# Upper and lower weight products of a chunk in two runs, and norm factors from one rounded product with ones

## The chip, the cores and the metric

The kernel runs on one core of one Trainium2 chip. The metric is the device time of one execution in microseconds, as the median of several runs.

## The reference

The reference is a decoder trunk of two layers over 256 tokens with 2,048 features, in float32. Layer 0 mixes tokens by attention in three dilation groups; layer 1 by a gated sum of compressed, selected-block and window attention, whose keys and values come from the stream after layer 0. After each mixer come an MLP and a gated per-layer embedding:

```
def rmsnorm(x, g):
    y = xf * lax.rsqrt(jnp.mean(xf * xf, axis=-1, keepdims=True) + NORM_EPS)
    return y * g
...
hn = rmsnorm(h, mlp_norm_g[i])
h = h + jnp.square(jax.nn.relu(hn @ mlp_w1[i])) @ mlp_w2[i]
gate = jax.nn.sigmoid(rmsnorm(h, ple_norm_g[i]) @ ple_w_gate[i])
h = h + (p[i] @ ple_w_proj[i]) * gate
```

Here `mlp_w1` is 2,048 x 8,192 and `mlp_w2` 8,192 x 2,048, in each of the two layers.

## The kernel before

The residual stream lies in SBUF feature-major: 16 tiles `x[k]` of 128 features x 256 tokens. All weights come in chunks of 128 x 1,024 float32, and nearly all of the work is multiplying chunks.

To keep float32 precision with rounded (fp32r) products, a weight is split in two: ACT casts the chunk to an upper part `hi` (line 197, tile `whi`) and DVE subtracts it from the raw chunk to make the lower part `lo` (line 203, tile `wlo`). Activations are split as well: a tile `xa` holds the upper half in columns 0 to 255 and the lower half in columns 256 to 511. A chunk is eight blocks of 128 x 128. For each block `mm_tile` issues two products: the upper weights with both halves of the activations (512 columns, line 321), and right behind it the lower weights with the upper half alone (256 columns, line 322). Every product has a weight load of its own. In PSUM a result so has two halves, which `sum_halves` (lines 326 and 328) adds.

Two helpers call `mm_tile`. `quad` takes chunks of two contraction blocks by four output blocks, and so fills four PSUM banks at once; `single` makes one output block from two chunks of eight contraction blocks each, all into one bank. PSUM has four banks named `mm` and two pairs named `at`, between which `four_banks` alternates. The last gate product (`one_half`, lines 376 to 378) uses 256-column products only. Two other helpers have loops of their own: `token_major` (lines 404 to 406), with 512-column products that move weights against activations as the loaded operand, and `compress` (lines 893 and 894), with 256-column ones. `both` lets chunks of these two alternate.

`Program.run` writes the order of all instructions by hand. For each chunk it issues loads (up to seven ahead), casts (four ahead), subtractions (three ahead), then one step of every generator under way, and then the chunk's products. A generator's `yield` means "go on at the next chunk"; `yield "tensor"` means "go on right behind this chunk's products". There are four raw buffers, six of `hi` and five of `lo`.

A norm is not applied to the activations but to the result, as a factor of each token. `Norm` adds up the squares of the 16 tiles into `acc` (128 partitions x 256 tokens); `factor` then makes a column of sums with two 1-column fp32 products (`column`, line 236), takes the root and inverts it on 128 x 2 elements (`root`, `invert`), writes the factors into a diagonal `diag`, spreads them over all partitions by an fp32 product with ones (`spread`, line 260), and copies them out as `r`. Four of the norms, those before the MLP and before the gate in each layer, enter as a hook behind the fifth chunk of the first `quad` that needs them; their results are used as `norm.rb`, first at line 464 (MLP) and line 550 (gate). The others go on to use the column and stay on `factor`.

Of the kernel before, what the change touches and what calls it, by code (L numbers as in the profile page):

```python
# [10 lines left out]
F32 = mybir.dt.float32  # L11
F32R = mybir.dt.float32r
AF = mybir.ActivationFunctionType
ALU = mybir.AluOpType

P = 128
D = 2048
T = 256
KT = D // P
DH = 128  # L20
EPS = 1e-6
# [19 lines left out]
def f32(ap):  # L41
    return ap.bitcast(F32)
# [90 lines left out]
def kernel(ctx: ExitStack, tc: tile.TileContext, a: dict, out: bass.AP):  # L133
    nc = tc.nc
# [3 lines left out]
    const = ctx.enter_context(tc.tile_pool(name="const", bufs=1))  # L138
    xpool = ctx.enter_context(tc.tile_pool(name="x", bufs=1))
    stat = ctx.enter_context(tc.tile_pool(name="stat", bufs=2))  # L140
    tmp = ctx.enter_context(tc.tile_pool(name="tmp", bufs=2))
# [4 lines left out]
    cur = {}  # L146
# [10 lines left out]
    def bank():  # L157
        return pspool.tile([P, 512], F32, tag="mm", name="mm", bufs=4)

    def banks2():  # L160
        return pspool.tile([P, 2, 512], F32, tag="at", name="at", bufs=2)
# [5 lines left out]
    x = [xp[k // 2][:, k % 2 * T:(k % 2 + 1) * T] for k in range(KT)]  # L167
    ones = const.tile([P, P], F32, name="ones")
    nc.vector.memset(ones, 1.0)
    ident = const.tile([P, P], F32, name="ident")  # L170
    ropeC = const.tile([32, T], F32, name="ropeC")
    ropeS = const.tile([32, T], F32, name="ropeS")
# [34 lines left out]
    class Norm:  # L207
# [51 lines left out]
        def spread(self, ps):  # L259
            nc.tensor.matmul(ps[:, 128:128 + T], ones, self.diag, start=True, stop=True)  # L260
            return ps[:, 128:128 + T]

        def factor(self, roped=False):
            while self.done < KT:
                yield
            yield "tensor"
            ps = self.column([self.acc])
            yield
            self.root(ps)
            yield  # L270
            self.invert()
            yield "tensor"
            rp = self.spread(ps)
            yield
            r = stat.tile([P, T], F32, tag="sr", name="sr", bufs=1)
            nc.scalar.copy(r, rp)
            if roped:
                yield
                self.rc = stat.tile([P, T], F32, tag="rc", name="rc", bufs=1)
                self.rs = stat.tile([32, T], F32, tag="rs", name="rs", bufs=1)  # L280
                nc.vector.tensor_mul(self.rs, r[:32, :], ropeS)
                nc.vector.tensor_copy(self.rc, r)
                nc.vector.tensor_mul(self.rc[:32, :], r[:32, :], ropeC)
            self.r = r
# [30 lines left out]
    def have(acts, k):  # L315
        prog.until(lambda: acts[k] is not None)
        return acts[k]

    def mm_tile(ps, hi, lo, col, rhs, first, last):

        nc.tensor.matmul(ps, hi[:, col:col + P], rhs, start=first, stop=False)  # L321
        nc.tensor.matmul(ps[:, :T], lo[:, col:col + P], rhs[:, :T], start=False, stop=last)  # L322

    def sum_halves(ps):
        s = tmp.tile([P, T], F32, tag="es", name="es", bufs=4)
# [5 lines left out]
    parity = [0]  # L331

    def four_banks():
        parity[0] ^= 1
        if parity[0]:
            return [bank() for _ in range(4)]
        return [p[:, i, :] for p in (banks2(), banks2()) for i in range(2)]
# [6 lines left out]
    def quad(src, nk, acts, done, hooks=None, single_ring=False, late=False):  # L344

        st = []
        for c in range(nk // 2):
            def step(hi, lo, c=c):
                if c == 0:
                    st.extend([bank() for _ in range(4)] if single_ring else four_banks())  # L350
                for i in range(2):
                    have(acts, 2 * c + i)
                for f in range(4):
                    for i in range(2):
                        k = 2 * c + i
                        mm_tile(st[f], hi, lo, i * 512 + f * P, acts[k], k == 0, k == nk - 1)
                if c < nk // 2 - 1:
                    return []
                return [delayed(done(f, st[f]), f // 2 if late else 0) for f in range(4)]
            prog.chunk(src(c), step)  # L360
            for fn in (hooks or {}).get(c, ()):
                prog.op(fn)

    def single(src, acts, done, mid=(), ring=bank, one_half=False):

        st = []
        for c in range(2):
            def step(hi, lo, c=c):
                if c == 0:
                    st.append(ring())  # L370
                for i in range(8):
                    k = 8 * c + i
                    if one_half:
                        xg, ps = have(acts, k), st[0][:, :T]
                        wh, wl = hi[:, i * P:(i + 1) * P], lo[:, i * P:(i + 1) * P]
                        nc.tensor.matmul(ps, wh, xg[:, :T], start=k == 0, stop=False)
                        nc.tensor.matmul(ps, wh, xg[:, T:], start=False, stop=False)
                        nc.tensor.matmul(ps, wl, xg[:, :T], start=False, stop=k == KT - 1)
                        continue
                    mm_tile(st[0], hi, lo, i * P, have(acts, k), k == 0, k == KT - 1)  # L380
                return [done(st[0])] if c else []
            prog.chunk(src(c), step)
            if c == 0:
                for fn in mid:
                    prog.op(fn)
# [69 lines left out]
    def mlp(layer, xg, norm, to, norm2):  # L455
        for b in range(NFB):
            h = [None] * 16
            for q in range(4):
                def done(f, ps, q=q, h=h):
                    t = sum_halves(ps)  # L460
                    yield
                    while norm.r is None:
                        yield
                    nc.vector.scalar_tensor_tensor(t, t, 0.0, norm.rb, op0=ALU.max, op1=ALU.mult)
                    yield
                    nc.scalar.activation(t, t, AF.Square)
                    ht = cur["h"].tile([P, 2 * T], F32R, tag="h", name="h", bufs=20)
                    yield from split_to(ht, t)
                    h[4 * q + f] = ht
                base = layer * 128 + (b * 4 + q) * 8  # L470
                quad(lambda c, base=base: a["w1"][base + c], KT, xg, done,
                     {4: [norm.factor]} if b == 0 and q == 0 else None, late=True)
            for q in range(4):
                def done(f, ps, q=q, b=b):
                    k = 4 * q + f
                    add_to_x(k, ps)
                    if b == NFB - 1:
                        yield
                        yield from renorm(k, G_PLE + layer, to, norm2)
                base = layer * 128 + (b * 4 + q) * 8  # L480
                quad(lambda c, base=base: a["w2"][base + c], 16, h, done, late=True)
# [10 lines left out]
    def ple(layer, pg, xg, norm, nxt, norm2, last):  # L492
# [80 lines left out]
        for q in range(4):  # L573
            def proj_done(f, ps, q=q):
                s = tmp.tile([P, T], F32, tag="es", name="es", bufs=4)
                nc.scalar.copy(s, ps[:, :T])
                t = cur["h"].tile([P, T], F32, tag="pj", name="pj", bufs=8)
                nc.vector.tensor_add(t, ps[:, T:], s)
                pj[4 * q + f] = t
                return  # L580
                yield
            quad(lambda c, q=q: a["w_proj"][layer * 4 + q], 2, pg, proj_done)
            hooks = {4: [norm.factor]} if q == 0 else {}
            if q == 3 and not last:
                for c in range(6):
                    hooks[c] = [lambda k=k: split_x(k, G_KV, nxt) for k in (2 * c, 2 * c + 1)]
            if q == 3 and last:
                for f in range(4):
                    single(lambda c, f=f: a["w_gl"][2 * f + c], xg,
                           (lambda ps, k=12 + f: gate_done(k, ps)) if f < 3 else last_gate,  # L590
                           ring=last_ring if f == 3 else lambda: banks2()[:, 0, :], one_half=f == 3)
            else:
                quad(lambda c, q=q: a["w_gate"][layer * 32 + q * 8 + c], KT, xg,
                     lambda f, ps, q=q: gate_done(4 * q + f, ps), hooks)
# [143 lines left out]
    hooks = {c: [lambda k=k: start_x(k) for k in (2 * c + 2, 2 * c + 3)] for c in range(7)}  # L738
# [3 lines left out]
    for h in range(HA):  # L742
        for i in range(6):
            single(lambda c, h=h, i=i: a["w_qk"][(h * 6 + i) * 2 + c], x_a0,
                   lambda ps, h=h, i=i: qk_done(h, i, ps),
# [423 lines left out]
    for h in range(HB):  # L1169
# [4 lines left out]
        if h:  # L1174
            prog.op(lambda h=h: b_scores(h - 1))
    hooks = {0: [lambda: b_pv(HB - 4, True), lambda: b_transpose(HB - 3)],
             1: [lambda: b_scores(HB - 1, banks2)],
             2: [lambda: b_pv(HB - 3, True), lambda: b_transpose(HB - 2)],
             4: [lambda: b_pv(HB - 2, True), lambda: b_transpose(HB - 1)],
             5: [lambda: b_pv(HB - 1, True)]}  # L1180
# [107 lines left out]
```

## Time and profile before

| | |
|---|---|
| median of 3 runs | 2519.74 us (2519.64 to 2519.77) |
| the profiled execution | 2519.91 us |
| its span, first to last instruction | 2518.1 us |
| granted TensorE clock, mean | 0.999 |
| busy: PE, PEld, DVE, ACT | 2507.3, 2204.1, 1716.8, 1342.8 us |
| read from HBM | 461.65 MB, 184 GB/s over the span |

PE is TensorE's matrix product, PEld its weight load, DVE the vector engine, ACT the scalar engine. Products are pipelined and overlap, so their busy time is not the time that each adds; the distance between two starts is.

### The profile page before, as it was taken

The numbers are of one execution on the slowest core, as the hardware profiler recorded it, in microseconds if no ns is written. First come the engines' busy times: TensorE is split into PE (matmuls) and PEld (weight loads), VectorE is DVE, ScalarE is ACT, GpSimd is POOL, SyncE is SP. The second block draws the span as 40 slices with busy tenths as digits, with TensorE's granted clock in tenths as the row PEclk, the third lists the DMA queues.
The fourth block names the chain that finished last, engine by engine and source line by source line (L and its number), as shares of the span: only waits on it lengthen the run. The fifth ranks groups of instructions, "written<-read, shape, count | busy, mean of one in ns | idle before, by whom it ended". The sixth has DMA issues, their size and how long they took to land.

```text
span 2518.1 us, 38042 instructions
## 1 busy us (share of the span) xinstructions
PE 2507.3 (100%) x14457; PEld 2204.1 (88%) x14457; DVE 1716.8 (68%) x3000; ACT 1342.8 (53%) x2152; POOL 10.4 (0%) x24
## 2 busy tenths in 40 slices
PE   9999999999999999999999999999999999999998
PEld 8888888888888888888888889888888888888887
DVE  6766677866565665567787989776556656556777
ACT  6444444554454453455564788655435445445555
POOL 0000000000000000000000000000000000000000
PEclk9999999999999999999999999999999999999999
DMA  7555555555555555555565743455555565555653
GB/s 268 173 180 178 175 161 180 176 188 189 193 188 190 192 190 189 190 191 189 185 199 190 248 155 125 141 191 185 192 190 188 191 191 188 190 192 188 190 185 124
DMA packets 130119, 466.23 MB, mean 185 GB/s; under 512 B 14608, under 2 KB 15888, under 8 KB 129936
## 3 DMA queue, kind: packets, MB, share of 16 engines
q1 hardware_dynamic: 129264, 462.68, 56.8%
q8 instruction: 113, 1.85, 0.3%
q0 software_dynamic: 528, 1.07, 0.2%
q14 instruction: 70, 0.57, 0.1%
q10 hardware_dynamic: 144, 0.07, 0.0%
HBM read 461.65 MB, written 2.10 MB: 184 GB/s over the span
## 4 chain that ended last, share of the span: by engine, by line
PE 99%; DVE 0%; DMA 0%; SPq 0%; ACT 0%; issue 0%; DVEq 0%
PE mm L321 31%; PE at L321 26%; PE mm L322 16%; PE at L322 14%; PE mm L404 1%; PE mm L406 1%; PE mm L405 1%; PE at L406 1%; PE at L404 1%; PE at L405 1%; PE at L1135 0%; PE at L673 0%; PE mm L1159 0%; PE mm L893 0%; PE mm L894 0%; DMA raw<-in_w_v 0%
## 5 line engine op out<-in xcount | busy, mean ns | idle before, releaser
L203 DVE TENSOR_TENSOR wlo<-raw,whi 128x1024 fp32r<-128x1024 f32 (+1 forms) x875 | 1065.5, 1219 | 624.8 <-PE at L322 242.1
L197 ACT CAST whi<-raw 128x1024 fp32r<-128x1024 f32 (+1 forms) x875 | 920.4, 1053 | 914.6 <-PE at L321 409.9
L321 PE MATMUL mm<-xa,whi 128*128 128x512 f32 x2176 | 765.1, 395 | 0.0
L322 PE MATMUL mm<-xa,wlo 128*128 128x256 f32 x2176 | 608.1, 279 | 0.0
L321 PE MATMUL at<-xa,whi 128*128 128x512 f32 x1648 | 573.6, 392 | 0.0
L321 PEld LDWEIGHTS mm<-xa,whi 128*128 128x128 f32 x2176 | 407.8, 187 | 91.9 <-issue 0.4
L322 PE MATMUL at<-xa,wlo 128*128 128x256 f32 x1648 | 461.1, 280 | 0.0
L322 PEld LDWEIGHTS mm<-xa,wlo 128*128 128x128 f32 x2176 | 410.6, 189 | 0.4
L321 PEld LDWEIGHTS at<-xa,whi 128*128 128x128 f32 x1648 | 308.3, 187 | 68.0
L321 PE MATMUL at<-h,whi 128*128 128x512 f32 x1024 | 355.7, 391 | 0.0
L321 PE MATMUL mm<-h,whi 128*128 128x512 f32 x1024 | 355.7, 391 | 0.0
L322 PEld LDWEIGHTS at<-xa,wlo 128*128 128x128 f32 x1648 | 311.3, 189 | 0.1
L322 PE MATMUL mm<-h,wlo 128*128 128x256 f32 x1024 | 286.7, 280 | 0.0
L322 PE MATMUL at<-h,wlo 128*128 128x256 f32 x1024 | 286.7, 280 | 0.0
L321 PEld LDWEIGHTS mm<-h,whi 128*128 128x128 f32 x1024 | 191.5, 187 | 42.0
L321 PEld LDWEIGHTS at<-h,whi 128*128 128x128 f32 x1024 | 191.5, 187 | 42.0
L322 PEld LDWEIGHTS mm<-h,wlo 128*128 128x128 f32 x1024 | 193.5, 189 | 0.0
L322 PEld LDWEIGHTS at<-h,wlo 128*128 128x128 f32 x1024 | 193.5, 189 | 0.0
L328 DVE TENSOR_TENSOR et<-mm,es 128x256 f32<-128x256 f32 x137 | 55.8, 422 | 80.3 <-ACT es L326 78.3
L326 ACT COPY es<-mm 128x256 f32<-128x256 f32 x137 | 48.2, 370 | 66.0 <-PE mm L322 63.0
L328 DVE TENSOR_TENSOR et<-at,es 128x256 f32<-128x256 f32 x103 | 43.5, 423 | 36.8 <-ACT es L326 31.3
L326 ACT COPY es<-at 128x256 f32<-128x256 f32 x103 | 37.8, 370 | 51.8 <-DVE et L328 40.5
(301 smaller groups left out, 2387.8 us busy)
## 6 DMA issues: line engine op xcount, KB each, us to landing
raw<-in_w SPq DMA_DIRECT2D x512, 512.0 KB, 3.5
raw<-in_w_qk SPq DMA_DIRECT2D x96, 512.0 KB, 3.7
raw<-in_w_gate SPq DMA_DIRECT2D x56, 512.0 KB, 3.6
raw<-in_w_kv SPq DMA_DIRECT2D x48, 512.0 KB, 4.2
raw<-in_w_v SPq DMA_DIRECT2D x46, 512.0 KB, 3.6
raw<-in_w_q SPq DMA_DIRECT2D x32, 512.0 KB, 4.4
raw<-in_w_oB SPq DMA_DIRECT2D x32, 512.0 KB, 3.6
raw<-in_w_oA SPq DMA_DIRECT2D x16, 512.0 KB, 3.6
```

The source lines that it names most:

```text
L197: nc.scalar.copy(hi[:, c], t[:, c])
L203: nc.vector.tensor_sub(lo[:, c], t[:, c], f32(hi)[:, c])
L321: nc.tensor.matmul(ps, hi[:, col:col + P], rhs, start=first, stop=False)
L322: nc.tensor.matmul(ps[:, :T], lo[:, col:col + P], rhs[:, :T], start=False, stop=last)
L326: nc.scalar.copy(s, ps[:, :T])
L328: nc.vector.tensor_add(t, ps[:, T:], s)
L404: nc.tensor.matmul(st[j], xh, wh, start=k == 0, stop=False)
L405: nc.tensor.matmul(st[j], xl, wh, start=False, stop=False)
L406: nc.tensor.matmul(st[j], xh, wl, start=False, stop=k == KT - 1)
```

## The change

`mm_tile` becomes `mm_tiles`: it takes a chunk's eight blocks as a list and issues all eight products with upper weights first, and then all eight with lower weights. `quad` and `single` hand it the list. `one_half`, `token_major` and `compress` stay as they are.

`factor_rows` is a new way to a norm's factors, for the four norms before the MLPs and the gates. It rounds `acc` on ACT and subtracts on DVE, so that one `h` tile holds an upper and a lower half of 256 columns; one product with a rounded 128 x 128 matrix of ones (512 columns) sums both over the partitions and leaves the sums on all of them; root and inverse are then taken on 128 x 256 elements.

```diff
--- before.py
+++ after.py
@@ -167,6 +167,8 @@
     x = [xp[k // 2][:, k % 2 * T:(k % 2 + 1) * T] for k in range(KT)]
     ones = const.tile([P, P], F32, name="ones")
     nc.vector.memset(ones, 1.0)
+    onesr = const.tile([P, P], F32R, name="onesr")
+    nc.gpsimd.memset(f32(onesr), 1.0)
     ident = const.tile([P, P], F32, name="ident")
     ropeC = const.tile([32, T], F32, name="ropeC")
     ropeS = const.tile([32, T], F32, name="ropeS")
@@ -260,6 +262,30 @@
             nc.tensor.matmul(ps[:, 128:128 + T], ones, self.diag, start=True, stop=True)
             return ps[:, 128:128 + T]
 
+        def factor_rows(self):
+
+            while self.done < KT:
+                yield
+            a = cur["h"].tile([P, 2 * T], F32R, tag="h", name="h", bufs=20)
+            nc.scalar.copy(a[:, :T], self.acc)
+            yield
+            nc.vector.tensor_sub(a[:, T:], self.acc, f32(a[:, :T]))
+            yield "tensor"
+            ps = banks2()[:, 0, :] if parity[0] else bank()
+            nc.tensor.matmul(ps, onesr, a, start=True, stop=True)
+            yield
+            v, z = (tmp.tile([P, T], F32, tag="et", name="et", bufs=7) for _ in range(2))
+            r = stat.tile([P, T], F32, tag="sr", name="sr", bufs=1)
+            nc.vector.tensor_scalar(z, ps[:, :T], 1.0 / D, EPS, op0=ALU.mult, op1=ALU.add)
+            nc.vector.scalar_tensor_tensor(v, ps[:, T:], 1.0 / D, z, op0=ALU.mult, op1=ALU.add)
+            nc.scalar.activation(z, v, AF.Sqrt)
+            yield
+            nc.vector.reciprocal(r, z)
+            nc.vector.tensor_mul(z, r, r)
+            nc.vector.scalar_tensor_tensor(z, z, -0.5, v, op0=ALU.mult, op1=ALU.mult)
+            nc.vector.scalar_tensor_tensor(r, z, 1.5, r, op0=ALU.add, op1=ALU.mult)
+            self.r = r
+
         def factor(self, roped=False):
             while self.done < KT:
                 yield
@@ -316,10 +342,16 @@
         prog.until(lambda: acts[k] is not None)
         return acts[k]
 
-    def mm_tile(ps, hi, lo, col, rhs, first, last):
-
-        nc.tensor.matmul(ps, hi[:, col:col + P], rhs, start=first, stop=False)
-        nc.tensor.matmul(ps[:, :T], lo[:, col:col + P], rhs[:, :T], start=False, stop=last)
+    def mm_tiles(hi, lo, tiles):
+
+
+
+
+
+        for ps, col, rhs, first, last in tiles:
+            nc.tensor.matmul(ps, hi[:, col:col + P], rhs, start=first, stop=False)
+        for ps, col, rhs, first, last in tiles:
+            nc.tensor.matmul(ps[:, :T], lo[:, col:col + P], rhs[:, :T], start=False, stop=last)
 
     def sum_halves(ps):
         s = tmp.tile([P, T], F32, tag="es", name="es", bufs=4)
@@ -350,10 +382,8 @@
                     st.extend([bank() for _ in range(4)] if single_ring else four_banks())
                 for i in range(2):
                     have(acts, 2 * c + i)
-                for f in range(4):
-                    for i in range(2):
-                        k = 2 * c + i
-                        mm_tile(st[f], hi, lo, i * 512 + f * P, acts[k], k == 0, k == nk - 1)
+                mm_tiles(hi, lo, [(st[f], i * 512 + f * P, acts[2 * c + i], 2 * c + i == 0, 2 * c + i == nk - 1)
+                                  for f in range(4) for i in range(2)])
                 if c < nk // 2 - 1:
                     return []
                 return [delayed(done(f, st[f]), f // 2 if late else 0) for f in range(4)]
@@ -368,6 +398,7 @@
             def step(hi, lo, c=c):
                 if c == 0:
                     st.append(ring())
+                tiles = []
                 for i in range(8):
                     k = 8 * c + i
                     if one_half:
@@ -377,7 +408,8 @@
                         nc.tensor.matmul(ps, wh, xg[:, T:], start=False, stop=False)
                         nc.tensor.matmul(ps, wl, xg[:, :T], start=False, stop=k == KT - 1)
                         continue
-                    mm_tile(st[0], hi, lo, i * P, have(acts, k), k == 0, k == KT - 1)
+                    tiles.append((st[0], i * P, have(acts, k), k == 0, k == KT - 1))
+                mm_tiles(hi, lo, tiles)
                 return [done(st[0])] if c else []
             prog.chunk(src(c), step)
             if c == 0:
@@ -469,7 +501,7 @@
                     h[4 * q + f] = ht
                 base = layer * 128 + (b * 4 + q) * 8
                 quad(lambda c, base=base: a["w1"][base + c], KT, xg, done,
-                     {4: [norm.factor]} if b == 0 and q == 0 else None, late=True)
+                     {4: [norm.factor_rows]} if b == 0 and q == 0 else None, late=True)
             for q in range(4):
                 def done(f, ps, q=q, b=b):
                     k = 4 * q + f
@@ -580,7 +612,7 @@
                 return
                 yield
             quad(lambda c, q=q: a["w_proj"][layer * 4 + q], 2, pg, proj_done)
-            hooks = {4: [norm.factor]} if q == 0 else {}
+            hooks = {4: [norm.factor_rows]} if q == 0 else {}
             if q == 3 and not last:
                 for c in range(6):
                     hooks[c] = [lambda k=k: split_x(k, G_KV, nxt) for k in (2 * c, 2 * c + 1)]
```

Behind the fifth chunk of its quad, the new generator issues the copy on ACT; at the next chunk the subtraction on DVE, and behind that chunk's products the product with ones; one chunk later two operations on DVE and the square root, and another chunk later the reciprocal and three more operations on DVE.

## The prediction

> **What bounds the kernel now.** I read the page first: busy times, the slices with the granted clock, the chain that ended last, then the costliest groups.
>
> ```profile
> span 2518.1 us, 38042 instructions
> PE 2507.3 (100%) x14457; PEld 2204.1 (88%) x14457; DVE 1716.8 (68%) x3000; ACT 1342.8 (53%) x2152; POOL 10.4 (0%) x24
> PEclk9999999999999999999999999999999999999999
> PE 99%; DVE 0%; DMA 0%; SPq 0%; ACT 0%; issue 0%; DVEq 0%
> PE mm L321 31%; PE at L321 26%; PE mm L322 16%; PE at L322 14%; PE mm L404 1%; PE mm L406 1%; PE mm L405 1%; PE at L406 1%; PE at L404 1%; PE at L405 1%; PE at L1135 0%; PE at L673 0%; PE mm L1159 0%; PE mm L893 0%; PE mm L894 0%; DMA raw<-in_w_v 0%
> ```
>
> TensorE is 99% of the chain at full granted clock, and lines 321 and 322, which the change reorders, are 87% of it. So the other engines matter only if they begin to hold TensorE up, and the question is what one TensorE product costs in each order. Busy time can't tell that, since products overlap (a 512-column one is "busy" for 391 ns and the next starts long before). I therefore work with starts: by source line, the first start, the last start and the count.
>
> ```profile
> L321 PE MATMUL mm<-h,whi x512: 391/391/391, 579.9 to 1178.6; 128*128 128x512 f32 x171
> L321 PE MATMUL at<-h,whi x509: 391/391/391, 602.1 to 1199.7; 128*128 128x512 f32 x170
> L321 PE MATMUL at<-xa,whi x448: 391/391/391, 557.7 to 1112.0; 128*128 128x512 f32 x150
> L321 PE MATMUL mm<-xa,whi x407: 391/391/391, 549.7 to 1089.8; 128*128 128x512 f32 x136
> ```
>
> In this stretch of the first MLP there are 1,876 pairs (upper product over 512 columns, then lower over 256) from 549.7 to 1199.7 us: 650.0 us / 1,875 = 346.7 ns a pair, with nothing lost in between. Eight pairs, one chunk, are 2,773 ns. The whole kernel has these pairs, by the same view without a window:
>
> ```profile
> L321 PE MATMUL mm<-xa,whi x2176: 389/392/586, 29.7 to 2292.1; 128*128 128x512 f32 x198
> L321 PE MATMUL at<-xa,whi x1648: 391/391/586, 513.1 to 2498.4; 128*128 128x512 f32 x184
> L321 PE MATMUL mm<-h,whi x1024: 391/391/391, 579.9 to 2380.8; 128*128 128x512 f32 x171
> L321 PE MATMUL at<-h,whi x1024: 391/391/391, 602.1 to 2403.0; 128*128 128x512 f32 x171
> L321 PE MATMUL mm<-ko,whi x128: 387/396/483, 1592.8 to 1669.4; 128*128 128x512 f32 x128
> L321 PE MATMUL at<-ko,whi x128: 387/396/403, 1624.7 to 1691.9; 128*128 128x512 f32 x128
> ...
> L321 PE MATMUL mm<-pg,whi x64: 391/391/580, 1201.1 to 2481.7; 128*128 128x512 f32 x64
> ```
>
> With the two groups left out (oT, 64 each) they sum to 6,320 pairs, that is 790 chunks.
>
> **Part one: eight upper, then eight lower.** Number, width and operands of the products stay; so do the weight loads, one a product. Only the neighbours change: 14 of 16 starts in a chunk will follow a product of the same width. The trace has runs of one width. Pure 512-column runs are the token-major products (three to each of the lines 404 to 406), and a pure 256-column run is the last gate product (lines 376 to 378):
>
> ```profile
> L404 PE MATMUL mm<-whi,xa x24: 389/389/389, 69.9 to 85.5; 128*128 128x512 f32 x24
> L404 PE MATMUL mm<-whi,xa x24: 389/389/389, 129.8 to 145.5; 128*128 128x512 f32 x24
> L376 PE MATMUL at<-xa,whi x16: 279/283/283, 2498.7 to 2504.1; 128*128 128x256 f32 x16
> ```
>
> Two runs of 69 gaps in 15.6 and 15.7 us give 226.8 ns for 512 columns; 45 gaps in 5.4 us give 120.0 ns for 256. Their sum, 346.8, is what a pair costs now in the steady MLP. So long runs of either kind would change nothing: no weight load is exposed in a run of 256-column products, which was my first fear.
>
> But a chunk's runs are only eight long, and the trace has a stretch with such short runs: from 1392 us the compression (eight 256-column products, lines 893 and 894) alternates with a token-major unit (twelve 512-column ones). The timeline of TensorE there, start first:
>
> ```profile
> 1399.45 0.29 PE L893 MATMUL mm<-whi,z 128*128 128x256 f32 x1
> ...
> 1400.42 0.39 PE L404 MATMUL at<-whi,xa 128*128 128x512 f32 x1
> ...
> 1401.58 0.39 PE L406 MATMUL at<-wlo,xa 128*128 128x512 f32 x1
> ...
> 1403.17 0.29 PE L893 MATMUL mm<-whi,z 128*128 128x256 f32 x1
> ...
> 1410.59 0.29 PE L893 MATMUL mm<-whi,z 128*128 128x256 f32 x1
> ```
>
> Three alternations take 1410.59 - 1399.45 = 11.14 us, 3,713 ns each. After a run of 256s the first five 512s are slow (1.16 us to the sixth, 232 ns each instead of 226.8), so the extra belongs to the change of width, not to the length of the run. Taking out four of the twelve at the settled 226.8 ns leaves 3,713 - 907 = 2,806 ns for eight and eight. Against 2,773 now that is **+33 ns a chunk**, and 790 x 33 = **+26.1 us**. Nothing hides it, since TensorE has no idle time there.
>
> The pairs are not everywhere as fast as in the MLP. In the two-chunk products and output projections some stretches run in a slower rhythm:
>
> ```profile
> 1522.81 0.40 PE L321 MATMUL mm<-xa,whi 128*128 128x512 f32 x1
> ...
> 1525.28 0.40 PE L321 MATMUL mm<-xa,whi 128*128 128x512 f32 x1
> ```
>
> That is seven pairs in 2.47 us, 352.9 ns each. There the new order, at 2,806 / 8 = 350.8, takes something back. These stages hold 134 chunks of two-chunk products (96 of w_qk, 32 of w_q, 6 of the last gate) and 384 pairs of output projection, 1,456 pairs in all; estimating that half of them are in the slow rhythm (bounds: none, all) gives 728 x 6.2 ns = **-4.5 us** (0 to -9.0).
>
> Weight readiness: the lower weights are needed eight products later than now, the upper ones at the same time, so no new wait on ACT or DVE. Bank release: the first bank of a four-bank group now ends after ten of a chunk's sixteen products, some 2.1 us into the last chunk instead of 0.7, so ACT's copy (line 326) and what is queued behind it on ACT, the next upper weights, start up to 1.4 us later. Those weights are made four chunks ahead and lower ones three, 8 us at 2.8 us a chunk, and the bank's next user comes two groups later; I cost it at nothing. Without that cover it would be at most 1.4 us a group.
>
> **Part two: four norms' sums.** The old route puts four short fp32 passes and two long ones on TensorE:
>
> ```profile
> 504.11 0.50 PE L236 MATMUL at<-ones,acc 128*128 128x1 f32 x4
> 504.47 0.48 PE L321 MATMUL mm<-xa,whi 128*128 128x512 f32 x1
> 504.78 0.28 PE L322 MATMUL mm<-xa,wlo 128*128 128x256 f32 x1
> ...
> 512.88 0.59 PE L260 MATMUL at<-diag,ones 128*128 128x256 f32 x2
> 513.12 0.59 PE L321 MATMUL at<-xa,whi 128*128 128x512 f32 x1
> 513.54 0.28 PE L322 MATMUL at<-xa,wlo 128*128 128x256 f32 x1
> ```
>
> From L236's first start to the lower product behind it are 0.67 us, where 0.23 would do: 0.44 us. For L260, 0.66 - 0.23 = 0.43 us. The new route has one rounded 512-column product, 0.23 us. Saved: 0.64 us a norm, four norms, **-2.6 us**. ACT swaps a 256-column copy into SBUF and a wider square root for a copy out of PSUM: about even. DVE gets more:
>
> ```profile
> L464 DVE SCALAR_TENSOR_TENSOR et<-et,sr 128x256 f32<-128x256 f32 x128 | 48.2, 418 | 0.0
> L1116 DVE RECIPROCAL sums<-sums 128x6 f32<-128x6 f32 x16 | 3.1, 192 | 0.6
> L249 DVE RECIPROCAL sy<-sz 128x2 f32<-128x2 f32 x7 | 1.1, 160 | 0.3 <-ACT sz L243 0.3
> 507.58 1.23 DVE L203 TENSOR_TENSOR wlo<-raw,whi 128x1024 fp32r<-128x1024 f32 x1 [1.93 <-ACT sz L243]
> ```
>
> Six operations at 0.42 us and a reciprocal over 256 columns, which by the two rows (32 ns for four more) I estimate at 2.2 us; 4.7 us over three chunks, with 1.2 us of splitting in each 2.8. It fits, and lower weights are three chunks ahead. The new product waits for DVE's subtraction, which stands a full chunk ahead of it; if that cover were gone, each norm would hold TensorE about 1.2 us, 5 us in all.
>
> **Sum.** The profiled execution took 2519.9 us (span 2518.1 plus 1.8), 0.2 over the median. 2519.9 + 26.1 - 4.5 - 2.6 = 2538.9; against the median **2538.7 us**, 0.75% slower. With the bounds above and 33 ns known to about 6 ns, this case spans 2530 to 2546.
>
> **A page's rule against it.** The Trainium skill, "TensorE: Matmul & The Clock Gate", section "Back-to-back issue gap", gives a product N / 2.4 + 2.5 ns alone, whatever stands before it, which by the page would be an estimated 325 ns a pair in either order. This trace disagrees on the size (346.7); whether order is free is the first rival.
>
> **Rivals.** First, **order is free**: each product costs its settled 226.8 or 120.0 ns wherever it stands, and the surplus in the alternation belongs to the compression itself. For it: the sum of the two settled rates equals today's pair. Against it: the slow five stand inside the token-major run. Then the slow rhythm goes too, and the time is 2519.7 - 4.5 - 2.6 = 2512.6, faster. It decides if the surplus is under 9 ns a chunk (7.1 us / 790). Chance 0.17, of which 0.04 ends within 0.2%.
>
> Second, **the upper run never settles**. One other run of 512s, sixteen products with activations moving as in the upper products, stays slow:
>
> ```profile
> 1460.19 2.95 PE L1036 MATMUL mm<-xa,pt 128*128 128x512 f32 x12
> ...
> 1463.90 0.39 PE L321 MATMUL mm<-xa,whi 128*128 128x512 f32 x1
> ```
>
> That is 3.71 us / 16 = 232 ns. Eight such and a 256 run (0.97 us, 1399.45 to 1400.42) make 2,826 ns, +53 a chunk, 790 x 53 = 41.9, so 2519.7 + 41.9 - 4.5 - 2.6 = 2554; half way to it, 2546. Chance 0.15. Third, **a norm holds TensorE** for the 5 us above: 2544, chance 0.05. The forecast case has 0.63.
>
> **How the numbers follow.** A measurement of this kernel tells about 0.2% (5 us) from no change. Left out of the range are the free order (0.17) and the last of the second rival: 2524 to 2550. Faster by over 0.2%: 0.13; within: 0.05; slower: 0.82.
>
> **What would show it.** In the profile after: starts of the upper line in the first MLP at 2.81 us a chunk instead of 2.77; in a chunk's timeline the first five upper products at 232 ns and the later ones at 227, lower ones at 120; the stretch from 1450 to 1700 us hardly longer; DVE and ACT as busy as before. A chunk at 2.77 us or less, or idle time of TensorE ahead of a lower product, would make it wrong.

## The result, and the profile after

| | before | after |
|---|---|---|
| median of 6 runs | 2519.76 us | 2528.96 us |
| range of the runs | 2519.64 to 2520.14 | 2528.80 to 2529.13 |
| profiled execution, its span | 2519.91, 2518.1 us | 2528.89, 2527.1 us |

The changed kernel is 9.2 us slower; the ratio is 1.0037 with a 95% interval of 1.0026 to 1.0047. The direction was forecast, but not the size: 2538.7 us had been expected, 19.0 us slower, and the loss is a little under half of that. The page of the changed kernel, where the upper products are line 352 and the lower ones line 354:

```profile
span 2527.1 us, 37986 instructions
PE 2515.6 (100%) x14437; PEld 2211.5 (88%) x14437; DVE 1719.9 (68%) x3000; ACT 1338.1 (53%) x2152; POOL 10.7 (0%) x25
PE 98%; DVE 1%; DMA 0%; ACT 0%; SPq 0%; issue 0%; DVEq 0%
```

TensorE still sets the time, at the same clock, and DVE and ACT are as busy as before. The starts of the upper products in the first MLP, by source line as in the prediction:

```profile
L352 PE MATMUL mm<-h,whi x512: 389/391/398, 578.8 to 1181.0; 128*128 128x512 f32 x171
L352 PE MATMUL at<-h,whi x501: 389/393/398, 601.1 to 1199.8; 128*128 128x512 f32 x167
L352 PE MATMUL at<-xa,whi x448: 389/391/398, 556.4 to 1113.9; 128*128 128x512 f32 x150
L352 PE MATMUL mm<-xa,whi x401: 389/389/398, 549.7 to 1091.6; 128*128 128x512 f32 x134
```

In the same 650 us there are 1,862 upper products where there were 1,876. A merged timeline gives the chunk itself (start and length in front, eight products to a row):

```profile
1017.33 2.00 PE L352 MATMUL at<-h,whi 128*128 128x512 f32 x8
1019.17 1.12 PE L354 MATMUL at<-h,wlo 128*128 128x256 f32 x8
1020.13 2.00 PE L352 MATMUL at<-h,whi 128*128 128x512 f32 x8
...
1028.51 2.00 PE L352 MATMUL mm<-xa,whi 128*128 128x512 f32 x8
```

Four chunks from 1017.33 to 1028.51 are 11.18 us. Over the whole MLP a chunk is 2,793.3 ns, against 2,773.3 before: **20 ns more**, not 33. The single starts in the trace show its shape: the distances from each product to the next are 234, 235, 229, 232, 231, 227, 226, 227 ns in the upper run, then 113 and seven times 120 in the lower run.

Where the 9 us lie follows from the start of the n-th upper product, which both kernels have in the same order; the last row goes to the end of the span:

| stage | upper products | before, us | after, us | difference |
|---|---|---|---|---|
| two-chunk products of layer 0 | 768 | 412.1 | 412.0 | -0.1 |
| output projection 0 | 128 | 48.1 | 47.8 | -0.4 |
| MLP 0 | 2,048 | 711.1 | 715.3 | +4.2 |
| embedding and gate 0 | 288 | 100.9 | 101.6 | +0.7 |
| shared keys and values | 256 | 152.4 | 153.4 | +0.9 |
| two-chunk products of layer 1 | 256 | 138.4 | 137.9 | -0.5 |
| output projection 1 | 256 | 99.4 | 99.1 | -0.3 |
| MLP 1 | 2,048 | 711.1 | 715.3 | +4.2 |
| embedding, gate 1 and the end | 272 | 114.7 | 115.4 | +0.6 |

An MLP has 256 chunks, and 256 x 20 ns = 5.1 us; the table has 4.2, since the new norm saves 0.7 there (by `e1_order_only` below, where the same stage is at +4.8).

There are also waits of TensorE that the kernel before did not have, by the list of who waited for whom (us in total, times, longest):

```profile
PE at L352 <- DVE x L470: 0.7, 2, 0.4
PE at L436 <- DVE et L360: 0.5, 1, 0.5
```

The first is at the first gate chunk of each layer, which here takes 1210.70 - 1207.28 = 3.42 us instead of 2.79 (the second is among the shared keys and values, at 1397.9 us):

```profile
1207.28 1.09 PE L352 MATMUL at<-xa,whi 128*128 128x512 f32 x4
1208.74 1.16 PE L352 MATMUL at<-xa,whi 128*128 128x512 f32 x4 [0.37 <-DVE x L470]
1209.74 1.12 PE L354 MATMUL at<-xa,wlo 128*128 128x256 f32 x8
1210.70 0.63 PE L352 MATMUL at<-xa,whi 128*128 128x512 f32 x2
```

The fifth product is the first into the third bank, which DVE still has to empty (line 470) from the MLP's last group.

### The profile page after: what moved, and what is told of

It reads as the page before. It is cut to its first block, busy times and chain, and to the rows that moved or that the text cites. A ratio compares the mean times of both kernels' runs of the same rounds, so it can differ in the third digit from the quotient of the medians.

```text
span 2527.1 us, 37986 instructions
## 1 busy us (share of the span) xinstructions
PE 2515.6 (100%) x14437; PEld 2211.5 (88%) x14437; DVE 1719.9 (68%) x3000; ACT 1338.1 (53%) x2152; POOL 10.7 (0%) x25
## 4 chain that ended last, share of the span: by engine, by line
PE 98%; DVE 1%; DMA 0%; ACT 0%; SPq 0%; issue 0%; DVEq 0%
PE mm L352 31%; PE at L352 26%; PE mm L354 16%; PE at L354 13%; PE mm L436 1%; PE mm L438 1%; PE mm L437 1%; PE at L438 1%; PE at L436 1%; PE at L437 1%; PE at L1167 0%; PE at L705 0%; PE mm L1191 0%; PE mm L925 0%; PE mm L926 0%; DMA raw<-in_w_v 0%
## 5 line engine op out<-in xcount | busy, mean ns | idle before, releaser
L352 PE MATMUL mm<-xa,whi 128*128 128x512 f32 x2176 | 548.2, 394 | 0.0
L352 PE MATMUL at<-xa,whi 128*128 128x512 f32 x1648 | 413.7, 393 | 0.7 <-DVE x L470 0.7
L354 PEld LDWEIGHTS mm<-xa,wlo 128*128 128x128 f32 x2176 | 296.8, 190 | 21.5
L354 PE MATMUL mm<-xa,wlo 128*128 128x256 f32 x2176 | 303.3, 282 | 0.0
L352 PE MATMUL at<-h,whi 128*128 128x512 f32 x1024 | 256.4, 392 | 0.0
L352 PE MATMUL mm<-h,whi 128*128 128x512 f32 x1024 | 256.4, 392 | 0.0
L354 PEld LDWEIGHTS at<-xa,wlo 128*128 128x128 f32 x1648 | 224.8, 190 | 16.1
L354 PE MATMUL at<-xa,wlo 128*128 128x256 f32 x1648 | 229.8, 282 | 0.0
L354 PE MATMUL at<-h,wlo 128*128 128x256 f32 x1024 | 142.8, 282 | 0.0
L354 PE MATMUL mm<-h,wlo 128*128 128x256 f32 x1024 | 142.8, 282 | 0.0
```

## Experiments: the two parts apart

My theory was the prediction's: the order costs TensorE some 20 ns a chunk, the norm part saves about 2.6 us, and the slow rhythm of the alternating order, where it occurs, is gone. The rival was that the parts have other signs than forecast. `e1_order_only` has the new order with the old factors:

```diff
-                     {4: [norm.factor_rows]} if b == 0 and q == 0 else None, late=True)
+                     {4: [norm.factor]} if b == 0 and q == 0 else None, late=True)
...
-            hooks = {4: [norm.factor_rows]} if q == 0 else {}
+            hooks = {4: [norm.factor]} if q == 0 else {}
```

> The new order of the products with the old norm factors. In the trace of the changed kernel a settled chunk of eight upper and eight lower products takes 2,793.3 ns against 2,773.3 before. If the order alone makes the loss and the new norm saves the forecast 2.6 us, this kernel takes 2528.96 + 2.6 = 2531.6 us. If the new norm saves nothing (or costs), 2529.0 us or less.

Measured: 2531.95 us (ratio to before 1.0048, 1.0035 to 1.0060). So in the new order the norm part saves 3.0 us, near the 2.6 forecast. `e2_norm_only` is the other half, the old order with `factor_rows`:

```diff
         for ps, col, rhs, first, last in tiles:
             nc.tensor.matmul(ps, hi[:, col:col + P], rhs, start=first, stop=False)
-        for ps, col, rhs, first, last in tiles:
             nc.tensor.matmul(ps[:, :T], lo[:, col:col + P], rhs[:, :T], start=False, stop=last)
```

> The old alternating order with the new norm factors. If the norm part saves what the prediction said, 2519.76 - 2.6 = 2517.2 us; if DVE's longer work holds TensorE up, 2519.8 us or more. A chunk in the first MLP should stay at 2,773 ns.

Measured: **2547.76 us** (1.0111, 1.0095 to 1.0126), 28 us slower than before, where the expectation had 2517.2 us, or 2519.8 and more if DVE held TensorE up. The MLP's starts in it (upper line 347):

```profile
L347 PE MATMUL mm<-h,whi x512: 395/398/403, 580.5 to 1190.7; 128*128 128x512 f32 x171
L347 PE MATMUL at<-h,whi x474: 395/398/403, 603.1 to 1199.9; 128*128 128x512 f32 x158
L347 PE MATMUL at<-xa,whi x448: 395/398/403, 557.9 to 1122.8; 128*128 128x512 f32 x150
L347 PE MATMUL mm<-xa,whi x407: 395/398/403, 549.7 to 1100.2; 128*128 128x512 f32 x136
```

Here 1,841 pairs take 650.2 us, 353.3 ns each: the slow rhythm that the prediction had seen in a few attention stretches now fills both MLPs. Around the norm's product (line 275):

```profile
506.39 0.40 PE L347 MATMUL mm<-xa,whi 128*128 128x512 f32 x1
...
506.76 0.39 PE L275 MATMUL at<-h,onesr 128*128 128x512 f32 x1
506.99 0.40 PE L347 MATMUL mm<-xa,whi 128*128 128x512 f32 x1
...
507.68 0.40 PE L347 MATMUL mm<-xa,whi 128*128 128x512 f32 x1
...
508.03 0.40 PE L347 MATMUL mm<-xa,whi 128*128 128x512 f32 x1
...
508.39 0.40 PE L347 MATMUL mm<-xa,whi 128*128 128x512 f32 x1
```

The two pairs from 507.68 on take 0.35 and 0.36 us; in single starts the rhythm is 241 and 120, 236 and 113, 233 and 117 ns, three pairs in 1,060 ns, over and over. It is there before the norm's product too, from the first pair of the MLP on (489.8 us; the output projection ahead of it has a repeat of its own, 349.0 ns a pair). The kernel before enters its MLP in the same slow rhythm; there the old norm's unrounded products followed (lines 236 and 260), and behind them the fast rhythm held.

That gave a second theory: the alternating order has a fast and a slow rhythm, and what TensorE ran just before decides which one holds until something interrupts it. Its rival was the norm's longer work on DVE and ACT, which might hold TensorE up.

## Experiments: what decides the rhythm

`e7_norm_fp32` keeps the old order and takes the norm's sums with one unrounded product, without the split:

```diff
-            a = cur["h"].tile([P, 2 * T], F32R, tag="h", name="h", bufs=20)
-            nc.scalar.copy(a[:, :T], self.acc)
-            yield
-            nc.vector.tensor_sub(a[:, T:], self.acc, f32(a[:, :T]))
+            yield
             yield "tensor"
...
-            nc.tensor.matmul(ps, onesr, a, start=True, stop=True)
+            nc.tensor.matmul(ps[:, :T], ones, self.acc, start=True, stop=True)
...
-            nc.vector.tensor_scalar(z, ps[:, :T], 1.0 / D, EPS, op0=ALU.mult, op1=ALU.add)
-            nc.vector.scalar_tensor_tensor(v, ps[:, T:], 1.0 / D, z, op0=ALU.mult, op1=ALU.add)
+            nc.vector.tensor_scalar(v, ps[:, :T], 1.0 / D, EPS, op0=ALU.mult, op1=ALU.add)
```

> Old alternating order; the four norms with one unrounded product of ones with the summed squares (256 columns, the form of the old spreading product) instead of the split and the rounded product; DVE and ACT work on 128 x 256 elements otherwise as in the changed kernel. The kernel with the old order and the rounded product took 2547.8 us because all MLP and gate chunks ran in the slow rhythm (353.3 ns a pair). If the rhythm is set by what TensorE ran just before, and an unrounded product resets it as the old one did, the MLP pairs are back at 346.7 ns and the time is 2519.8 - 4 x 0.44 = 2518.0 us. If DVE's longer work on the norm made it slow, it stays near 2547.

Measured: 2517.50 us (0.9991, 0.9982 to 1.0000), 30 us less than with the rounded product; a chunk is 2,773.3 ns again. This kernel also has less work on DVE and ACT, so `e10_reset` adds to the slow kernel, `e2_norm_only`, and takes nothing away:

```diff
-            ps = banks2()[:, 0, :] if parity[0] else bank()
+            wide = banks2() if parity[0] else None
+            ps, spare = (wide[:, 0, :], wide[:, 1, :]) if parity[0] else (bank(), bank())
             nc.tensor.matmul(ps, onesr, a, start=True, stop=True)
+            nc.tensor.matmul(spare[:, :T], ones, self.acc, start=True, stop=True)
```

> The kernel with the old order and the rounded norm product (2547.8 us), with one more thing: right behind each of the four rounded products an unrounded product of ones with the summed squares (256 columns) into a spare bank that nobody reads. It adds work: 0.44 us each, 1.8 us. If the rhythm of the alternating order is set by what TensorE ran just before, the MLP chunks fall from 2,827 to 2,773 ns and the time to about 2519 us in spite of the added work. If the norm's longer chain on DVE and ACT made it slow, 2549.5 us.

Measured: 2518.61 us (0.9994, 0.9984 to 1.0003). Four useless products make the kernel 29 us faster. The first of them (line 277, in its two passes), and the starts of the MLP's upper products behind it:

```profile
506.98 0.39 PE L276 MATMUL at<-h,onesr 128*128 128x512 f32 x1
507.21 0.59 PE L277 MATMUL at<-acc,ones 128*128 128x256 f32 x2
507.45 0.58 PE L349 MATMUL mm<-xa,whi 128*128 128x512 f32 x1
...
507.98 0.40 PE L349 MATMUL mm<-xa,whi 128*128 128x512 f32 x1
...
509.03 0.39 PE L349 MATMUL mm<-xa,whi 128*128 128x512 f32 x1
```

```profile
L349 PE MATMUL mm<-h,whi x512: 392/394/395, 579.7 to 1178.4; 128*128 128x512 f32 x171
L349 PE MATMUL at<-h,whi x510: 392/394/395, 601.9 to 1199.9; 128*128 128x512 f32 x170
L349 PE MATMUL at<-xa,whi x448: 392/394/395, 557.6 to 1111.9; 128*128 128x512 f32 x150
L349 PE MATMUL mm<-xa,whi x406: 392/394/395, 549.9 to 1089.7; 128*128 128x512 f32 x136
```

These are 1,876 pairs in 650.0 us, as many as in the kernel before: 346.7 ns a pair, 2,773.3 ns a chunk. DVE's and ACT's chain is the same as in `e2_norm_only`; that rival has fallen.

Not every unrounded product does it. In the kernel before, the one-column products (line 236) at both gates leave the pairs slow, and only the 256-column product (line 260) three chunks later makes them fast. The first gate:

```profile
1217.74 0.50 PE L236 MATMUL mm<-ones,acc 128*128 128x1 f32 x4
...
1218.54 0.40 PE L321 MATMUL at<-xa,whi 128*128 128x512 f32 x1
...
1219.60 0.40 PE L321 MATMUL at<-xa,whi 128*128 128x512 f32 x1
```

That is three pairs in 1.06 us, where the fast rhythm takes 1.04 (1.05 in the rows of line 277 above, to their hundredths). Behind line 260 the pairs are fast all six times in that trace, behind line 236 two times of six, both of them in an MLP's first chunks. The 256-column product also leaves a gap (the first pair behind it takes 0.53 us), and no run separates the gap from the kind of product.

## Experiments: what a change of width costs

The kernels here are the changed one with runs of another length. `e3_runs4` cuts a chunk's eight into runs of four; `e5_runs2` has a 2 in each place of the 4:

```diff
-        for ps, col, rhs, first, last in tiles:
-            nc.tensor.matmul(ps, hi[:, col:col + P], rhs, start=first, stop=False)
-        for ps, col, rhs, first, last in tiles:
-            nc.tensor.matmul(ps[:, :T], lo[:, col:col + P], rhs[:, :T], start=False, stop=last)
+        for n in range(0, 8, 4):
+            for ps, col, rhs, first, last in tiles[n:n + 4]:
+                nc.tensor.matmul(ps, hi[:, col:col + P], rhs, start=first, stop=False)
+            for ps, col, rhs, first, last in tiles[n:n + 4]:
+                nc.tensor.matmul(ps[:, :T], lo[:, col:col + P], rhs[:, :T], start=False, stop=last)
```

> The changed kernel, but each chunk in two halves: four upper products, four lower, four upper, four lower. If every change of width and back costs 20 ns whatever the length of the runs, a chunk is 2,813 ns and the kernel 2529.0 + 15.8 = 2544.8 us. If the cost is a transient over the first five upper products that a run of four cuts short (the first four are 24 ns over in the changed kernel, 7 ns come back at the change down), a chunk is some 2,807 ns: 2540. If the 20 ns come once a chunk, with its new weights, the time stays at 2529.0. If short runs fall back into the locked rhythm of the alternating order, a chunk is 2,773 ns and the time 2513.

> The changed kernel with runs of two: two upper products, two lower, four times a chunk. A settled chunk is 2,773.3 ns in the old order, 2,793.3 in runs of eight, 2,807 in runs of four. If the cost is a transient that begins at each change to the wide products (first two 16 ns over, about 7 ns back at the change down), a chunk is some 2,811 ns in the MLPs and the kernel about 2540 us. If the shortest runs lock into a rhythm of their own as the alternating order does, it is 2,773 (2513 us) or, in the slow rhythm of the kernel with the old order and new norm, 2,827 (2556 us).

`e4_serpentine` turns every second chunk round, so that runs are sixteen long (`upper` and `lower` are lists of the chunk's products):

```diff
+        turn[0] = 0 if tiles[0][3] else 1 - turn[0]
...
+        for ps, w, rhs, first, last in (lower + upper if turn[0] else upper + lower):
+            nc.tensor.matmul(ps, w, rhs, start=first, stop=last)
```

> The changed kernel, but every second chunk of a product takes its lower weights first, so that runs of sixteen follow each other and there is half the number of changes of width; products, operands and chunks are the same. If the change of width costs 20 ns each time there and back, a chunk is 2,783 ns on average: 2529.0 - 7.9 = 2521.1 us. If the 20 ns come with each chunk and its new weights, the time stays at 2529.0.

Their timelines in the first MLP, `e3_runs4`, `e5_runs2` and `e4_serpentine` in this order:

```profile
800.80 1.09 PE L348 MATMUL at<-h,whi 128*128 128x512 f32 x4
801.73 0.64 PE L350 MATMUL at<-h,wlo 128*128 128x256 f32 x4
802.21 1.09 PE L348 MATMUL at<-h,whi 128*128 128x512 f32 x4
...
806.41 1.09 PE L348 MATMUL mm<-h,whi 128*128 128x512 f32 x4
```

```profile
800.48 0.63 PE L348 MATMUL at<-h,whi 128*128 128x512 f32 x2
800.95 0.39 PE L350 MATMUL at<-h,wlo 128*128 128x256 f32 x2
801.18 0.62 PE L348 MATMUL mm<-h,whi 128*128 128x512 f32 x2
...
803.27 0.63 PE L348 MATMUL mm<-h,whi 128*128 128x512 f32 x2
```

```profile
803.78 3.82 PE L357 MATMUL mm<-h,whi 128*128 128x512 f32 x16
807.43 2.08 PE L357 MATMUL mm<-h,wlo 128*128 128x256 f32 x16
809.35 3.82 PE L357 MATMUL mm<-h,whi 128*128 128x512 f32 x16
```

In these rows two chunks of four-runs are 806.41 - 800.80 = 5.61 us, one chunk of two-runs 803.27 - 800.48 = 2.79, two chunks in runs of sixteen 809.35 - 803.78 = 5.57. Over the whole MLP, by single starts, beside a settled chunk of the alternating order:

| runs of | chunk in the MLP, ns | over, a chunk | over, each change there and back | kernel, us (ratio, interval) |
|---|---|---|---|---|
| 1, slow rhythm | 2,826.7 | 53.3 | 6.7 | 2547.76, `e2_norm_only` |
| 1, fast rhythm | 2,773.3 | 0 | 0 | 2518.61, `e10_reset` |
| 2 (`e5_runs2`) | 2,786.7 | 13.3 | 3.3 | 2522.43 (1.0010, 1.0001 to 1.0020) |
| 4 (`e3_runs4`) | 2,806.7 | 33.3 | 16.7 | 2536.25 (1.0065, 1.0052 to 1.0078) |
| 8, the change | 2,793.3 | 20.0 | 20.0 | 2528.96 |
| 16 (`e4_serpentine`) | 2,783.3 | 10.0 | 20.0 | 2521.37 (1.0006, 0.9998 to 1.0015) |

Runs of sixteen came out as the cost of a change foretold (2521.1), which rules out a cost of each chunk or of its new weights. Runs of four have the chunk that the cut-short transient gave (2,807), but the kernel was 4 us under the time for it, as the stages outside the MLPs lost less (the two-chunk products of layer 1 take 137.9 us, as in the changed kernel). Runs of two fit none of the expectations: 2,787 ns lies between the lock and the transient.

Then the difference in price: why had the alternation of compression and token-major units 33 ns, and the chunks only 20? `e6_compress_runs` tests whether it was the same loaded operand `zl` twice running:

```diff
-                for i in range(4):
-                    zl = z[:, 4 * (c % 2) + i].rearrange("p a g n -> p (a g n)")
-                    cols = slice(i * 256, (i + 1) * 256)
-                    nc.tensor.matmul(st[0], zl, hi[:, cols], start=c == 0 and i == 0, stop=False)
-                    nc.tensor.matmul(st[0], zl, lo[:, cols], start=False, stop=c == 7 and i == 3)
+                for w in (hi, lo):
+                    for i in range(4):
+                        zl = z[:, 4 * (c % 2) + i].rearrange("p a g n -> p (a g n)")
+                        nc.tensor.matmul(st[0], zl, w[:, i * 256:(i + 1) * 256], start=c == 0 and i == 0 and w is hi,
+                                         stop=c == 7 and i == 3 and w is lo)
```

> The changed kernel, with the compression's eight products of a chunk in another order: four blocks with upper weights, then the same four with lower ones, so that no weights are loaded twice running. Read in the stretch where it alternates with twelve token-major products: 3,713 ns an alternation before, of which 33 ns over the settled rates, where the changed kernel's own chunks have 20. If the repeated load made the alternation dearer than the chunks, it falls to about 3,700 ns; if not, it stays at 3,713. The total hardly moves either way: 2528.7 to 2529.0 us.

```profile
1401.32 0.65 PE L925 MATMUL mm<-whi,z 128*128 128x256 f32 x4
...
1408.74 0.65 PE L925 MATMUL mm<-whi,z 128*128 128x256 f32 x4
```

Two alternations in 7.42 us: 3,713 in single starts, nothing has moved. It is not the repeated load. (The one execution of this kernel took 2529.53 us, where 2528.7 to 2529.0 had been expected.) `e9_two_by_two` doubles both run lengths and leaves the operands:

```diff
-        for i in range(max(len(one), len(two))):
-            prog.steps += one[i] if i < len(one) else []
-            prog.steps += two[i] if i < len(two) else []
+        for i in range(0, max(len(one), len(two)), 2):
+            for part in (one, two):
+                for s in part[i:i + 2]:
+                    prog.steps += s
```

> The changed kernel, with the chunks of compression and token-major units taken two by two, so that runs of sixteen 256-column products alternate with runs of twenty-four 512-column ones, in place of eight and twelve. At the settled rates an alternation is 24 x 226.7 + 16 x 120.0 = 7,360 ns. If the surplus of a change there and back depends on the length of the wide run (twelve gave 33 ns, eight and sixteen 20), it is about 20 here: 7,380 ns. If it depends on what these products read (weights moving, activations held), it stays at 33: 7,393 ns. The total hardly moves: 2528 to 2530 us.

```profile
1403.80 0.29 PE L925 MATMUL mm<-whi,z 128*128 128x256 f32 x1
...
1411.18 0.29 PE L925 MATMUL mm<-whi,z 128*128 128x256 f32 x1
...
1418.56 0.29 PE L925 MATMUL mm<-whi,z 128*128 128x256 f32 x1
```

Two alternations of sixteen and twenty-four take 14.76 us, 7,380 ns each: 20 ns over the settled rates. (The one execution took 2528.50 us.) So with the same operands the lengths of the runs alter the surplus. Which of the two lengths matters, and by what rule, is not settled, since both were doubled. Nor does it clear the kind of operand, although the chunks have 20 as well, for the two are made up differently. In single starts, the first wide products here take 233 and 231 ns and then the settled 227, 11 ns over, and the way back costs 9: the last wide product takes 232 ns, the first narrow one 124. A chunk is 28 over at the start and gets some 7 back (227 and 113). The dear way back stays with the alternation's products at both lengths; what makes it so is open.

## An experiment for a faster version

`e8_turns_in_attention` is `e7_norm_fp32` with runs of sixteen in the two-chunk products and output projections only, where the alternating order had often been slow; `mm_turns` is the function of `e4_serpentine`:

```diff
-                mm_tiles(hi, lo, tiles)
+                mm_turns(hi, lo, tiles)
                 return [done(st[0])] if c else []
...
             quad(lambda c, q=q: src[q * (nk // 2) + c], nk, oT, done, hooks if q == 0 else None,
-                 single_ring and q == 0, True)
+                 single_ring and q == 0, True, mm_turns)
```

> The kernel before this one in the list (old order in the MLPs, gates and shared keys, unrounded norm product), with runs of sixteen (every second chunk lower weights first) in the two-chunk products and output projections, where the alternating order often falls into the slow rhythm. Runs of sixteen cost 2,783 ns a chunk against 2,773 in the fast rhythm and 2,827 in the slow one. If half of those pairs are in the slow rhythm the gain is 182 chunks x 17 ns = 3 us: 2515. If the MLPs' rhythm is upset by the other way in, 28 us more: 2543.

Measured: **2515.53 us** (0.9983, 0.9974 to 0.9992), 4.2 us under the kernel before and 13.4 under the changed one. Of the 4.2, 2.2 are the unrounded norm (`e7_norm_fp32`, 2517.50) and 2.0 the runs of sixteen, where 3 had been expected. The MLP chunks are at 2,773.3 ns. Its page:

```profile
span 2513.7 us, 37950 instructions
PE 2502.9 (100%) x14441; PEld 2193.6 (87%) x14441; DVE 1723.3 (69%) x2992; ACT 1341.6 (53%) x2148; POOL 10.7 (0%) x25
```

## Why the prediction was right in sign and wrong in size

- **What bounds it**: right. TensorE is 98% of the chain after, and no engine became the bound.
- **Weight loads hidden in a run of 256s**: right; the lower run settles at 120 ns.
- **The step that failed is the +33 ns a chunk**, a term of the right kind and the wrong size. I took the price of a change of width from runs of eight and twelve, of other operands, and used it for eight and eight. In single starts those 33 ns are 26 in the first five wide products and 7 on the way back (232 and 124 ns where settled rates give 227 and 120); the prediction spoke of the five alone. In the chunks the slow start was as foreseen (234, 235, 229, 232, 231 ns, 28 over), but on the way back they get some 7 back (227 and 113). The price is 20 ns, and 790 x 20 = 15.8 us stand in the place of 26.1. Why the way back is cheap in the chunks stays open: `e9_two_by_two` brings the alternation to 20 ns too, but by a cheaper start, with the way back as dear as before. I had given the 33 an uncertainty of 6, the reading error, when the step that needed a margin was the carrying over.
- **Slow rhythm recovered, -4.5 us**: about right. The two-chunk products and output projections have 176 chunks; at 20 ns each they would have lost 3.5 us and in the stage table gained 1.3, so some 4.8 us came back. That half of those pairs are slow was a guess, and a good one: away from interruptions they take 349.8 ns on average, between 346.7 and 353.3. What it meant I had not seen: the rhythm was a state of the order, and the kernel before depended on being in the fast one.
- **The norms, -2.6 us**: right in the new order, 3.0 by `e1_order_only`. Taken alone the same part costs 28 us, through the rhythm.
- **Bank release at nothing**: wrong by a little. I said that a bank's next user comes two groups later, at 8 us; but at the gate the group between is the one-chunk embedding product, and TensorE stops there, 0.6 us in each layer by the chunk's length. There is a wait of 0.5 us at line 436 besides.

The sum as measured: +15.8 - 4.8 - 3.0 + 1.7 = +9.7, against 9.2. Of the 0.5 us left over, 0.3 lie ahead of the first upper product, which starts at 29.4 us instead of 29.7: a wait of 0.4 us for lower weights (line 406, at 13.7 us) is gone there, whether by the change or by chance.

The measured time lies under the 2530 to 2546 us that the prediction gave its own case. (Its bounds, 4.5 us for the slow rhythm and 790 x 6 ns = 4.7 us for the price, plainly added give 2529.5 to 2547.9.) That the wider 2524 to 2550 holds it is luck: no row was named for its lower end.

The first rival, a free order, is refuted for this order (20 ns a chunk, not 0). The rule of the Trainium skill, "TensorE: Matmul & The Clock Gate", section "Back-to-back issue gap", which gives the gap of a product alone from its own width and is set apart there from a stream of loads and products, does not carry over to this stream: the same 16 products take 2,773, 2,787, 2,793, 2,807 or 2,827 ns by their order and by what ran before. The second rival, an upper run that never settles, did not occur in the MLPs, where it settles at 227 ns. The third, a norm that holds TensorE, did not occur either: line 275, the norm's product, is not in the list of TensorE's waits.

## What to carry to other kernels

When TensorE is full, read the distances between starts and look for the pattern they repeat; a stretch of products of mixed widths can hold different rates, and an edit elsewhere can throw it from one into the other. Before an edit is judged by the total, take its parts apart: here the norm part was worth -3 us in one order and +28 in the other. A price read from a neighbouring stretch should be carried over only with the lengths and the sequence that it was read at.

## What was not expected of the hardware

Alternating 512- and 256-column products, each with a weight load, ran in the MLPs at 346.7 or 353.3 ns a pair for hundreds of microseconds on end, with the same operands, clock and waits. One unrounded product of 256 columns in front was enough to bring the fast rate. These are not all the rhythms: the first output projection runs at 349.0 ns a pair (three pairs in 1,047), and the second passes between 346.7 and 353.3 with no other product in between (351.4 on average), so that a rhythm does not always last until something interrupts it. The surplus of a change of width there and back was 0, 3.3, 16.7, 20 and 20 ns for runs of one (fast), two, four, eight and sixteen, 33 for eight and twelve, and 20 for sixteen and twenty-four. What in TensorE keeps the rhythm was not found: the waits of TensorE in `e2_norm_only` and `e10_reset` are the same, and the weight loads in the MLP take 187 to 190 ns in both. It stays open.
